# Stick-breaking heads: three places of scores and a look-ahead of two units, one shared bank for two outputs, projections in 256-token pieces through one bank

## The chip, the core and the metric

The kernel runs on one core of one Trainium2 chip. The metric is the device time of one execution in microseconds (us). The kernel before was run three times: 2854.28, 2857.3 and 2858.99 us, median 2857.3. The names of the engines in every profile line are: PE = TensorE (matrix products), PEld = its weight loads, DVE = VectorE, ACT = ScalarE, POOL = GpSimd, SP = SyncE, which issues DMAs.

## The reference

One decoder layer, 2048 tokens of width 1024, float32. One projection feeds eight stick-breaking heads of width 64 and four differential heads; then come an output projection and a SwiGLU feed-forward block. What the change touches is the first kind of head:

```python
h = rmsnorm(x, attn_norm_g[layer])
proj = h @ w_in[layer]
sb_q, sb_k, sb_v, d_q, d_k, d_v = jnp.split(proj, [...])
...
def stick_breaking_attention(q, k, v):
    for start in range(0, S, Q_BLOCK):
        end = start + Q_BLOCK
        z = einsum('bhqd,bhkd->bhqk', q[:, :, start:end], k[:, :, :end]) * scale
        past = arange(end)[None, :] < arange(start, end)[:, None]
        log_beta = log_sigmoid(z)
        log_1m = where(past, log_sigmoid(-z), 0.0)
        acc = cumsum(log_1m, axis=3, reverse=True) - log_1m
        w = where(past, exp(log_beta + acc), 0.0)
        outs.append(einsum('bhqk,bhkd->bhqd', w, v[:, :, :end]))
```

Each weight is a sigmoid times the product of the (1 - beta) of all later keys. The kernel takes the product itself with a scan that runs from the last key backwards, and it carries the running product from one block of keys to the earlier one.

## The kernel before

Every product of two float32 matrices is done with each factor split into a high and a low half-precision part: `mm3` gives three matmuls (high x high, high x low, low x high) into one PSUM sum. The heads are worked in groups of two: groups 0 to 3 are stick-breaking, groups 4 to 7 differential (`SBP` is 4).

**Units.** A stick-breaking group has 40 units. A unit (`unit_sb`) is 128 queries against a block of up to 512 keys, for both heads. Its `scores` are 6 matmuls of 512 columns on PE into a place of 1024 float32 columns of PSUM. Its `main` has three sigmoids on ScalarE (L800 all of beta, L801 and L802 the two halves of 1 - beta; L802 writes back into PSUM), on VectorE two scans (L805) and a product (L808, the last reader of the score place), then a small carry (L813), and on GpSimd a large product (L816). Two units later ScalarE casts the weights to their high part (L829), three units later VectorE makes the low part (L834), both are transposed by DMA, and six units after its `main` PE multiplies two units' weights with v (`values`). At the end of a row of blocks `store` reads the output place (L869 on ScalarE, L870 on VectorE).

**PSUM.** It has eight banks of 512 float32 columns, and is one tile, `psum`, of 4096 columns. The table `places` (L237) gives, for each mode, the columns of the scores ("z"), of projections ("pj") and of outputs ("av"); `place` takes them in turn. The mode is "first" while the input is read, "sb" through groups 0 to 3, "next" from the first projection of a differential group on (set in `project_diff`), "leave" from unit 9 of group 4 and "diff" from its unit 12.

**Projections as filler.** While a group's units run, q, k and v of the next group (or of this one's later tokens) are made between them. `project_sb` makes them for 512 tokens in one place: q 24 matmuls of 512 columns, k the same, v 96 of 128 columns. It is a generator: each `yield` is a point at which it can be left, and `yield END` ends a piece. A finished piece is evacuated by `halved`, ScalarE first (L544, high part) and VectorE behind it (L545, low part from PSUM and the high part), which `clock.at(1, ..., "mid")` puts into the next unit, behind that unit's `main`.

**The order of one unit** in the main loop, the same on all engines since each engine takes its instructions in program order: outputs and stores that are due, `main(n)`, the evacuations ("mid"), the casts and other due work, then `look_ahead(n)`, which puts out scores up to unit n + 1 for stick-breaking groups (n + 2 for differential ones), and then at most one piece of projections if the plan wants PE work by now (`short`). Before the first scores of a new group, what is left of the filler for it is put out, with `tick()` running the due work between pieces.

Of the kernel before, what the change touches and what calls it, by code (L numbers as in the profile page):

```python
# [18 lines left out]
KB = D // 128  # L19
# [5 lines left out]
SBP = 4  # L25
# [39 lines left out]
def hybrid_layer_kernel(  # L65
# [23 lines left out]
    clock = Ticks()  # L89
# [79 lines left out]
    def mm3(ps, lh, ll, rh, rl, first, last):  # L169
        mm(ps, lh, rh, first, False)  # L170
        mm(ps, lh, rl, False, False)
        mm(ps, ll, rh, False, last)
# [52 lines left out]
    with ExitStack() as actx:  # L225
# [9 lines left out]


        places = {  # L237
# [5 lines left out]
        mode, turn = ["first"], {}  # L243

        def place(kind, w):
            if kind == "av1":

                turn[kind] = 128 - turn.get(kind, 0)
                n = turn[kind] + (3840 if turn["pj"] % 2 == 0 else 3328)
                return psum[:, n:n + w]  # L250
            ps = places[mode[0]][kind]
            n = turn[kind] = (turn.get(kind, -1) + 1) % len(ps)
            return psum[:, ps[n]:ps[n] + w]
# [4 lines left out]
        h_hi = hT_p.tile([128, KB, S], F16, name="h_hi")  # L258
        h_lo = hT_p.tile([128, KB, S], F16, name="h_lo")
# [131 lines left out]
        qkv = {g: {} for g in range(NG)}  # L391

        END, DONE = "end", "done"
# [28 lines left out]
        def pj_tile(name):  # L422
            return place("pj", 256)
# [23 lines left out]
        def bank_totals():  # L447
            while totals:
                sp, then = totals.pop(0)

                def read(sp=sp, then=then):
                    sp.take()
                    chain.extend(sp.steps())
                    clock.at(2, then)

                sp.total(pj_tile("tot")[:, 0:1])
                clock.at(1, read, "ev")
                yield END
# [84 lines left out]
        def halved(ps, hi, lo):  # L543
            nc.scalar.activation(hi, ps, AF.Copy, scale=OUT_SC)  # L544
            nc.vector.scalar_tensor_tensor(lo, ps, OUT_SC, hi, ALU.mult, ALU.subtract)  # L545

        def by_parity(k):

            return k.rearrange("p (r n) -> p r n", r=2)

        def project_sb(c, g):


            cs = slice(c * 512, (c + 1) * 512)
            q = qp.tile([128, 2, 2, 512], F16, tag="q", name="q")[:, 0]
            k = kp.tile([128, 2, 512], F16, tag="k", name="k")
            v = vp.tile([128, 4, 2, 128], F16, tag="v", name="v")
            yield from weights(g)
            ws = wsl[g]
            for t in range(2):  # L560
                yield from bank_totals()
                ps, w2 = place("pj", 512), ws[t]
                for kk in range(KB):
                    mm3(ps, w2[:, 0, kk, :], w2[:, 1, kk, :], h_hi[:, kk, cs], h_lo[:, kk, cs],
                        kk == 0, kk == KB - 1)
                    if kk % 2 == 1 and kk < KB - 1:
                        yield

                def evac(ps=ps, t=t):
                    if t == 0:  # L570
                        halved(ps, q[:, 0], q[:, 1])
                    else:
                        halved(ps.rearrange("p (n r) -> p r n", r=2), by_parity(k[:, 0]),
                               by_parity(k[:, 1]))

                clock.at(1, evac, "mid")
                yield END
            yield from bank_totals()
            w2 = ws[2]
            ps = place("pj", 512).rearrange("p (j n) -> p j n", j=4)  # L580
            for j in range(4):

                ts = slice(c * 512 + j // 2 * 256 + j % 2, c * 512 + j // 2 * 256 + 256, 2)
                for kk in range(KB):
                    mm3(ps[:, j, :], h_hi[:, kk, ts], h_lo[:, kk, ts], w2[:, 0, kk, :],
                        w2[:, 1, kk, :], kk == 0, kk == KB - 1)
                if j < 3:
                    yield

            def evac_v():  # L590
                halved(ps, v[:, :, 0, :], v[:, :, 1, :])
                qkv[g][c] = (q, k, v)

            clock.at(1, evac_v, "mid")
            yield END

        staged, roping = [0], [False]

        def project_diff(c, g):
            q = qp.tile([128, 2, 2, 512], F16, tag="q", name="q")  # L600
            k = kp.tile([128, 2, 512], F16, tag="k", name="k")
            v = vp.tile([128, 4, 2, 128], F16, tag="v", name="v")
            yield from weights(g)
            ws = wsl[g]
            if mode[0] == "sb":
                mode[0] = "next"
            while not settle():
                yield END
            while staged[0] == 2:
# [36 lines left out]
            r = {}  # L646
# [568 lines left out]
        def look_ahead(n):  # L1215

            while ahead[0] < len(plan):
                g = plan[ahead[0]][0]
                if ahead[0] > n + (1 if g < SBP else 2):
                    break  # L1220
                if g > 0 and ahead[0] > 0 and plan[ahead[0] - 1][0] != g:
                    for _ in fills[g - 1]:
                        tick()
                plan[ahead[0]][1]()
                ahead[0] += 1
# [4 lines left out]
        for n, (g, scores, front, main, goal, due) in enumerate(plan):  # L1230
            if g != g0:
                base, fbase, g0, since = pe[0], filled[0], g, 0
            since += 1
            if g == SBP and since in (9, 12):
                mode[0] = "leave" if since == 9 else "diff"
            clock.run("ev")
            if front is not None and (n == 0 or plan[n - 1][0] != g):
                front()
            if n + 1 < len(plan) and plan[n + 1][0] == g and plan[n + 1][2] is not None:
                plan[n + 1][2]()  # L1240
            for kind in ("", "main", "mid", None):
                main() if kind == "main" else clock.run(kind)

            def short():
                return pe[0] - base < goal or filled[0] - fbase < due

            look_ahead(n)
            if g == NG - 1 and since == 18:
                late[0] = True
            left = 1 if g + 1 < NG else 2  # L1250
            while left and short() and (n + 2 >= len(plan) or plan[n + 2][0] == g):
                more = fill_next(g)
                if more is DONE:
                    break
                left -= more == END
            clock.step()
# [511 lines left out]
```

## Time and profile before

| what | value |
|---|---|
| median of three runs | 2857.3 us |
| the profiled execution, its own time | 2850.8 us |
| its span, from the first to the last instruction | 2849.0 us |
| mean granted TensorE clock, share of full speed | 0.96 |
| stage: input and first projections | about 0 to 83 us |
| stage: stick-breaking groups 0 to 3 | 83 to 751 us |
| stage: differential groups 4 to 7 | 751 to about 1440 us |
| stage: output projection and norm, then feed-forward | about 1440 us to the end |

A line of a group or timeline view names the line of the kernel, the engine, the operation and `out<-in` by the program's tile names. In the timeline a row begins with its start in us and its duration, and a bracket gives the wait ahead of it and who ended it. In the table of waits a row reads: who waits, for whom, then the sum in us, the number of waits and the longest. In the view by stretches, each engine's busy time is followed by its number of instructions in brackets, and then come the granted clock, the DMA engines' mean busy share and GB/s. The releaser is the semaphore that came last; it is inferred.

### The profile page before, as it was taken

How to read it: one execution, taken by the hardware profiler on the slowest of the kernel's cores; microseconds unless marked ns; L12 is line 12 of the kernel's file. 1: busy time of each engine (PE TensorE's matmuls, PEld its weight loads, DVE VectorE, ACT ScalarE, POOL GpSimd, SP SyncE). 2: the span in 40 equal slices, each digit the busy share in tenths (PEclk: the TensorE clock that was granted, in tenths of full speed). 3: DMA queues.
4: the chain of work that ended last, by engine and by line, in shares of the span. 5: the costliest groups of instructions: out<-in, count | busy, mean ns of one | idle time of the engine just before them, and what ended most of it. 6: DMA issues, size and time to landing. Idle time of an engine off the chain costs nothing.

```text
span 2849.0 us, 50446 instructions
## 1 busy us (share of the span) xinstructions
PE 2527.5 (89%) x19626; PEld 1462.0 (51%) x19626; DVE 2304.0 (81%) x3561; ACT 1549.2 (54%) x2603; POOL 1400.7 (49%) x1099
## 2 busy tenths in 40 slices
PE   6978888897786887877998999999999999999999
PEld 4534445455575666765853444444444444444444
DVE  7898989888889888988748688988777767776776
ACT  5788888886565766565415444545433433343332
POOL 2454545547656565564124555655444544454442
PEclk9989999998898998998998999999999999999999
DMA  4576878866555556668766122122217521112111
GB/s 160 92 146 119 147 138 141 142 129 123 103 94 99 98 105 116 130 120 181 171 159 148 65 100 85 64 78 78 71 45 148 163 89 45 45 49 85 45 45 74
DMA packets 734096, 301.49 MB, mean 106 GB/s; under 512 B 618656, under 2 KB 713120, under 8 KB 733856
## 3 DMA queue, kind: packets, MB, share of 16 engines
q1 hardware_dynamic: 733712, 298.23, 46.4%
q8 instruction: 153, 2.51, 0.4%
q14 instruction: 87, 0.71, 0.1%
q0 software_dynamic: 144, 0.03, 0.0%
HBM read 127.27 MB, written 28.31 MB: 55 GB/s over the span
## 4 chain that ended last, share of the span: by engine, by line
PE 45%; DVE 20%; ACT 6%; POOL 5%; issue 5%; DMA 4%; SPq 1%; DVEq 0%; ACTq 0%; POOLq 0%
PE pw L167 34%; PE psum L167 11%; DMA wt<-wh 2%; DVE fs L1376 2%; DVE mx L178 2%; DVE acc_a L1633 2%; DVE wh L178 1%; DVE pp L178 1%; DVE hh L1420 1%; DVE pp L805 1%; DVE wh L834 1%; ACT pp L930 1%; POOL sc L1550 1%; DVE wmx L105 1%; DVE rt L681 1%
## 5 line engine op out<-in xcount | busy, mean ns | idle before, releaser
L167 PE MATMUL pw<-t,fs 128*128 128x512 f16 x3696 | 808.5, 381 | 15.7 <-issue 10.3
L167 PEld LDWEIGHTS <-fs 128*128 128x128 f16 x3696 | 360.6, 98 | 454.6 <-issue 17.1
L816 POOL TENSOR_TENSOR pp<-pp 128x1024 f32<-128x1024 f32 (+1 forms) x160 | 325.1, 2032 | 317.5 <-DVE pp L813 137.3
L167 PE MATMUL pw<-acc_b,at 128*128 128x512 f16 x2112 | 463.3, 379 | 18.2 <-DVE cg L1558 11.9
L167 PE MATMUL psum<-k,q 64*128 64x512 f16 (+4 forms) x1600 | 288.6, 377 | 152.2 <-DVE pp L808 79.2
L167 PE MATMUL psum<-ws,h_hi 128*128 128x128 f16 x4096 | 377.7, 224 | 21.4 <-ACT psum L1008 12.0
L167 PE MATMUL psum<-ws,h_lo 128*128 128x128 f16 x2048 | 366.9, 224 | 0.0
L167 PEld LDWEIGHTS <-h_hi 128*128 128x128 f16 x4096 | 328.6, 101 | 51.3 <-issue 40.1
L167 PEld LDWEIGHTS <-at 128*128 128x128 f16 x2112 | 205.7, 98 | 267.9 <-issue 22.7
L1561 POOL TENSOR_TENSOR cg<-cg,cu 128x512 f32<-128x512 f32 x88 | 112.4, 1277 | 371.1 <-ACT cg L1560 336.9
L1375 ACT ACTIVATE fs<-acc_b,fst 128x512 f16<-128x512 f32 x264 | 176.1, 714 | 216.8 <-POOL acc_b L1364 143.6
L1633 DVE SCALAR_TENSOR_TENSOR acc_a<-pw,isd,acc_a 128x512 f32<-128x512 f32 x352 | 248.8, 745 | 53.8 <-PE pw L167 53.2
L1376 DVE SCALAR_TENSOR_TENSOR fs<-acc_b,fst,fs 128x512 f16<-128x512 f32 x264 | 248.4, 981 | 31.8 <-ACT fs L1375 31.7
L1550 POOL TENSOR_TENSOR sc<-sc 128x512 f32<-128x512 f32 x132 | 220.0, 1683 | 91.5 <-ACT sc L1544 91.5
L805 DVE TENSOR_TENSOR_SCAN pp<-pp,psum 128x256 f32<-128x256 f32 (+1 forms) x320 | 195.8, 653 | 57.7 <-ACT psum L802 57.0
L167 PEld LDWEIGHTS <-q 64*128 64x128 f16 (+1 forms) x1600 | 94.7, 99 | 260.8 <-DVE pp L808 103.8
L1544 ACT COPY sc<-pw 128x512 f32<-128x512 f32 x176 | 100.4, 582 | 217.9 <-PE pw L167 191.4
L834 DVE TENSOR_TENSOR wh<-pp,wh 128x1024 f16<-128x1024 f32 (+1 forms) x160 | 205.9, 1287 | 2.6 <-DMA wt<-wh 2.6
L167 PEld LDWEIGHTS <-h_lo 128*128 128x128 f16 x2048 | 206.3, 101 | 0.0
L930 ACT ACTIVATE pp<-psum,nb,ds_sc 128x1024 f32<-128x1024 f32 (+4 forms) x192 | 183.1, 954 | 18.8 <-DVE pp L178 9.6
L178 DVE TENSOR_REDUCE mx<-psum 128x1 f32<-128x1024 f32 (+4 forms) x192 | 173.6, 905 | 24.1 <-PE psum L167 21.3
L800 ACT ACTIVATE pp<-psum,gsc 128x1024 f32<-128x1024 f32 (+1 forms) x160 | 164.8, 1030 | 36.4 <-PE psum L167 32.4
(211 smaller groups left out, 4456.2 us busy)
## 6 DMA issues: line engine op xcount, KB each, us to landing
acc_b<-in_w_gate_dram SPq DMA_DIRECT2D x22, 1024.0 KB, 5.2
acc_b<-in_w_up_dram SPq DMA_DIRECT2D x22, 1024.0 KB, 7.5
acc_b<-in_w_down_dram SPq DMA_DIRECT2D x22, 1024.0 KB, 9.5
raw<-in_w_in_dram SPq DMA_DIRECT2D x24, 512.0 KB, 4.3
pp<-in_x_dram SPq DMA_DIRECT2D x16, 512.0 KB, 5.2
wt<-wh SPq DMA_TRANSPOSE x512, 3.2
raw<-in_w_o_dram SPq DMA_DIRECT2D x16, 512.0 KB, 4.1
mt<-mix_d SPq DMA_DIRECT2D x32, 256.0 KB, 3.2
```

Of the source, the lines that this page charges most:

```text
L167: nc.tensor.matmul(ps, lhsT=lhsT, rhs=rhs, start=start, stop=stop)
L178: fn(*a, **k)
L800: nc.scalar.activation(be, z[:, :, 0:W], AF.Sigmoid, scale=sc[:, 0:1])
L805: nc.vector.tensor_tensor_scan(ga, ga, z[:, h, P:W][:, ::-1], 2.0 ** 14 if diag else cx[a][:, h, 0:1], ALU.mult, ALU.mult)
L816: nc.gpsimd.tensor_mul(b4, b4, gp[:, :, 1:P + 1].rearrange("p h (r n) -> p h r n", r=1).to_broadcast([128, 2, 2, P]))
L834: nc.vector.tensor_sub(wl[:, 0:n], b2, u["wh"][:, 0:n])
L930: nc.scalar.activation(pt, u["z"][:, 0:e - b], AF.Exp, scale=ds_sc, bias=nb[:, m:m + 1], accum_out=su[:, jj:jj + 1])
L1375: nc.scalar.activation(w[:, m, 0:4], src, AF.Copy, scale=sw)
L1376: nc.vector.scalar_tensor_tensor(w[:, m, 4:8], src, sw, w[:, m, 0:4], ALU.mult, ALU.subtract)
L1550: nc.gpsimd.tensor_add(s[m], s[m], y[m])
L1561: nc.gpsimd.tensor_mul(g, g, u)
L1633: nc.vector.scalar_tensor_tensor(acc[:, i, hs], ps, pr.isd, acc[:, i, hs], ALU.mult, ALU.add)
```

## The change

The table of places loses the modes "next" and "leave". In mode "sb" the scores have three places of two banks (columns 0, 1024 and 2048), the projections have the two halves of one bank (columns 3072 and 3328), and the outputs the two halves of the last (3584 and 3840). The input's mode has four half-bank places for projections instead of two whole ones. `look_ahead` runs two units ahead in all groups, and mode "diff" begins at unit 9 of group 4. `project_sb` makes q, k and v in two pieces of 256 tokens each, with an `END` and an evacuation for each piece, so a call has six pieces instead of three. Lines from 237 on move by -2, and lines of `unit_sb` by +2, so L800, L802, L805, L808 are L802, L804, L807, L810 afterwards, and L544 and L545 are L542 and L543.

```diff
@@ -235,10 +235,8 @@
 
 
         places = {
-            "first": {"z": [0, 1024, 2048], "pj": [3072, 3584]},
-            "sb": {"z": [0, 1024], "pj": [2048, 2560], "av": [3072, 3584]},
-            "next": {"z": [0, 1024], "pj": [2048, 2560, 2304, 2816], "av": [3072, 3584]},
-            "leave": {"z": [0, 1024], "pj": [3072, 3584]},
+            "first": {"z": [0, 1024, 2048], "pj": [3072, 3584, 3328, 3840]},
+            "sb": {"z": [0, 1024, 2048], "pj": [3072, 3328], "av": [3584, 3840]},
             "diff": {"z": [0, 1024, 2048], "pj": [3072, 3584]}}
         mode, turn = ["first"], {}
 
@@ -558,41 +556,47 @@
             yield from weights(g)
             ws = wsl[g]
             for t in range(2):
+                for u in range(2):
+                    yield from bank_totals()
+                    ps, w2 = pj_tile("pj"), ws[t]
+                    us = slice(c * 512 + u * 256, c * 512 + u * 256 + 256)
+                    for kk in range(KB):
+                        mm3(ps, w2[:, 0, kk, :], w2[:, 1, kk, :], h_hi[:, kk, us],
+                            h_lo[:, kk, us], kk == 0, kk == KB - 1)
+                        if kk == KB // 2 - 1:
+                            yield
+
+                    def evac(ps=ps, t=t, u=u):
+                        if t == 0:
+                            halved(ps, *(q[:, y, u * 256:u * 256 + 256] for y in range(2)))
+                        else:
+                            halved(ps.rearrange("p (n r) -> p r n", r=2),
+                                   *(by_parity(k[:, y])[:, :, u * 128:u * 128 + 128]
+                                     for y in range(2)))
+
+                    clock.at(1, evac, "mid")
+                    yield END
+            w2 = ws[2]
+            for u in range(2):
                 yield from bank_totals()
-                ps, w2 = place("pj", 512), ws[t]
-                for kk in range(KB):
-                    mm3(ps, w2[:, 0, kk, :], w2[:, 1, kk, :], h_hi[:, kk, cs], h_lo[:, kk, cs],
-                        kk == 0, kk == KB - 1)
-                    if kk % 2 == 1 and kk < KB - 1:
+                ps = pj_tile("pj").rearrange("p (j n) -> p j n", j=2)
+                for j in range(2):
+
+                    ts = slice(c * 512 + u * 256 + j, c * 512 + u * 256 + 256, 2)
+                    for kk in range(KB):
+                        mm3(ps[:, j, :], h_hi[:, kk, ts], h_lo[:, kk, ts], w2[:, 0, kk, :],
+                            w2[:, 1, kk, :], kk == 0, kk == KB - 1)
+                    if j == 0:
                         yield
 
-                def evac(ps=ps, t=t):
-                    if t == 0:
-                        halved(ps, q[:, 0], q[:, 1])
-                    else:
-                        halved(ps.rearrange("p (n r) -> p r n", r=2), by_parity(k[:, 0]),
-                               by_parity(k[:, 1]))
-
-                clock.at(1, evac, "mid")
+                def evac_v(ps=ps, u=u):
+                    js = slice(2 * u, 2 * u + 2)
+                    halved(ps, v[:, js, 0, :], v[:, js, 1, :])
+                    if u == 1:
+                        qkv[g][c] = (q, k, v)
+
+                clock.at(1, evac_v, "mid")
                 yield END
-            yield from bank_totals()
-            w2 = ws[2]
-            ps = place("pj", 512).rearrange("p (j n) -> p j n", j=4)
-            for j in range(4):
-
-                ts = slice(c * 512 + j // 2 * 256 + j % 2, c * 512 + j // 2 * 256 + 256, 2)
-                for kk in range(KB):
-                    mm3(ps[:, j, :], h_hi[:, kk, ts], h_lo[:, kk, ts], w2[:, 0, kk, :],
-                        w2[:, 1, kk, :], kk == 0, kk == KB - 1)
-                if j < 3:
-                    yield
-
-            def evac_v():
-                halved(ps, v[:, :, 0, :], v[:, :, 1, :])
-                qkv[g][c] = (q, k, v)
-
-            clock.at(1, evac_v, "mid")
-            yield END
 
         staged, roping = [0], [False]
 
@@ -602,8 +606,6 @@
             v = vp.tile([128, 4, 2, 128], F16, tag="v", name="v")
             yield from weights(g)
             ws = wsl[g]
-            if mode[0] == "sb":
-                mode[0] = "next"
             while not settle():
                 yield END
             while staged[0] == 2:
@@ -1216,7 +1218,7 @@
 
             while ahead[0] < len(plan):
                 g = plan[ahead[0]][0]
-                if ahead[0] > n + (1 if g < SBP else 2):
+                if ahead[0] > n + 2:
                     break
                 if g > 0 and ahead[0] > 0 and plan[ahead[0] - 1][0] != g:
                     for _ in fills[g - 1]:
@@ -1231,8 +1233,9 @@
             if g != g0:
                 base, fbase, g0, since = pe[0], filled[0], g, 0
             since += 1
-            if g == SBP and since in (9, 12):
-                mode[0] = "leave" if since == 9 else "diff"
+            if g == SBP and since == 9:
+
+                mode[0], turn["pj"] = "diff", 0
             clock.run("ev")
             if front is not None and (n == 0 or plan[n - 1][0] != g):
                 front()
```

Three places show how this changes the order on the engines. In each row stand the line, the operation, `out<-in` and the shape; a bracket names the semaphores that it waits for. First PE, near the end of group 0, where the scores of a unit (from `k,q`) are followed by a piece of a projection (from `h_hi`, `h_lo` and the weights `ws`). Before:

```order
L167 LDWEIGHTS q
L167 MATMUL psum<-k,q 128x512
L167 LDWEIGHTS ws
L167 MATMUL psum<-h_hi,ws 128x512
L167 LDWEIGHTS ws
L167 MATMUL psum<-h_lo,ws 128x512
```

And the changed kernel at the same place:

```order
L167 LDWEIGHTS q
L167 MATMUL psum<-k,q 128x512
L167 LDWEIGHTS ws
L167 MATMUL psum<-h_hi,ws 128x256 [waits DVE_49]
L167 LDWEIGHTS ws
L167 MATMUL psum<-h_lo,ws 128x256
```

The piece has half the columns, and its first matmul has a wait for VectorE that was not there. The second place is VectorE at the end of group 0; `q`, `k`, `v` are evacuations, `pp` and `wh` the units' work. Before, the last evacuation of this stretch:

```order
L805 SCALAR_TENSOR_TENSOR pp<-pp,psum 128x256 x2
L808 TENSOR_TENSOR pp<-pp,psum 128x2x256
L834 TENSOR_TENSOR wh<-pp,wh 128x1024
L813 TENSOR_REDUCE pp<-pp 128x2
L545 SCALAR_TENSOR_TENSOR v<-psum,v 128x4x128
```

And in the changed kernel, two units of the same stretch:

```order
L810 TENSOR_TENSOR pp<-pp,psum 128x2x256
L836 TENSOR_TENSOR wh<-pp,wh 128x1024
L815 TENSOR_REDUCE pp<-pp 128x2
L543 SCALAR_TENSOR_TENSOR q<-psum,q 128x256
L807 SCALAR_TENSOR_TENSOR pp<-pp,psum 128x256 x2
L810 TENSOR_TENSOR pp<-pp,psum 128x2x256
L836 TENSOR_TENSOR wh<-pp,wh 128x1024
L815 TENSOR_REDUCE pp<-pp 128x2
L543 SCALAR_TENSOR_TENSOR k<-psum,k 128x2x128
```

The evacuation that PE's next piece waits for stands, as before, behind the scans and the product of the unit in which it is put out; there are now two for every 512 tokens of q, k or v. The third place is ScalarE in the same stretch, the sigmoids of a unit, what stands behind them, and the next unit's first sigmoid. Before:

```order
L800 ACTIVATE pp<-psum,gsc 128x1024 [waits DVE_49,PE_49]
L801 ACTIVATE pp<-psum,gsc 128x2x256 [waits DVE_49]
L802 ACTIVATE psum<-psum,gsc 128x2x256 [waits Activation_49]
L544 ACTIVATE q<-psum 128x512 [waits PE_49]
L829 CAST wh<-pp 128x1024 [waits DMAHW1_49,Pool_49]
L800 ACTIVATE pp<-psum,gsc 128x1024 [waits DVE_49,PE_49]
```

And in the changed kernel:

```order
L802 ACTIVATE pp<-psum,gsc 128x1024 [waits DVE_49,PE_49]
L803 ACTIVATE pp<-psum,gsc 128x2x256 [waits DVE_49]
L804 ACTIVATE psum<-psum,gsc 128x2x256 [waits Activation_49]
L542 ACTIVATE q<-psum 128x256 [waits PE_49]
L831 CAST wh<-pp 128x1024 [waits DMAHW5_49,Pool_49]
L802 ACTIVATE pp<-psum,gsc 128x1024 [waits DVE_49]
```

The order on ScalarE is the same, with a piece's evacuation ahead of the cast and of the next unit's sigmoids. The last rows are the end of group 0 in the changed kernel, where the pieces of group 1 that are left over are put out between the last sigmoids of group 0 and the first of group 1:

```order
L542 ACTIVATE k<-psum 128x2x128 [waits DVE_49,PE_49]
L831 CAST wh<-pp 128x1024 [waits DMAHW1_49,Pool_49]
L871 ACTIVATE mxs<-psum 128x256 [waits PE_49]
L831 CAST wh<-pp 128x1024 [waits DMAHW3_49,Pool_49]
L542 ACTIVATE k<-psum 128x2x128 [waits DVE_49,PE_49]
L831 CAST wh<-pp 128x1024 [waits DMAHW5_49,Pool_49]
L542 ACTIVATE v<-psum 128x2x128 [waits DVE_49,PE_49] x2
L802 ACTIVATE pp<-psum,gsc 128x1024
```

Three pieces (the second `k` and two of `v`) stand there with no unit between them; before, every piece of group 1 was put out between units.

## The prediction

> **What bounds the kernel now.** I read the page first, then busy time by stretch for the four groups of stick-breaking heads, then the table of waits for the same stretch, then the timeline inside it.
>
> ```profile
> span 2849.0 us, 50446 instructions
> PE 2527.5 (89%) x19626; PEld 1462.0 (51%) x19626; DVE 2304.0 (81%) x3561; ACT 1549.2 (54%) x2603; POOL 1400.7 (49%) x1099
> 83.00:239.00 156.00, 126.48 (x1203) 71.03 (x1200) 138.36 (x249) 131.06 (x183) 79.54 (x39) 0.92 0.68 124
> 239.00:398.00 159.00, 134.42 (x1283) 75.08 (x1283) 143.59 (x246) 131.77 (x184) 79.92 (x40) 0.92 0.74 138
> 398.00:551.00 153.00, 130.17 (x1283) 75.02 (x1283) 140.16 (x242) 131.10 (x184) 80.49 (x41) 0.96 0.79 142
> 551.00:751.00 200.00, 159.81 (x1906) 110.55 (x1907) 171.46 (x280) 140.10 (x204) 116.93 (x70) 0.90 0.71 128
> ```
>
> The four stretches (columns after the length: PE, PEld, DVE, ACT, POOL busy, granted clock, DMA share, GB/s) are groups 0 to 3, 40 units each, 668 us together. The shares of the page do not hold here: over the whole span PE is the busy engine, but in these stretches it is VectorE, with 138.4 + 143.6 + 140.2 + 171.5 = 593.6 us of 668. VectorE idles 74 us; that is the most that any smoothing could win. What it waits for:
>
> ```profile
> PE psum L167 <- DVE pp L808: 79.2, 50, 5.5
> DVE pp L805 <- ACT psum L802: 57.0, 49, 4.6
> ACT pp L800 <- PE psum L167: 32.4, 28, 5.1
> ACT q L544 <- PE psum L167: 15.6, 6, 4.2
> ACT v L544 <- PE psum L167: 11.9, 8, 3.3
> ACT k L544 <- PE psum L167: 8.5, 5, 3.0
> PE psum L167 <- DVE v L545: 3.1, 4, 1.2
> ```
>
> 57 of the 74 us are waits for the third sigmoid (L802), and ScalarE in turn waits 68 us for PE: 32.4 us for scores and 36.0 us for projections that it is to evacuate. PE waits for VectorE's last read of a score place (L808), and almost never (3.1 us) for an evacuation. How a late projection becomes a late sigmoid stands in ScalarE's rows where pieces are dense:
>
> ```profile
> 200.55 1.04 ACT L829 CAST wh<-pp 128x1024 f16<-128x1024 f32 x1
> 201.49 1.12 ACT L800 ACTIVATE pp<-psum,gsc 128x1024 f32<-128x1024 f32 x1
> 202.50 0.69 ACT L801 ACTIVATE pp<-psum,gsc 128x512 f32<-128x512 f32 x1
> 203.22 0.66 ACT L802 ACTIVATE psum<-psum,gsc 128x512 f32<-128x512 f32 x1
> 206.39 0.60 ACT L544 ACTIVATE v<-psum 128x512 f16<-128x512 f32 x1 [2.51 <-PE psum L167]
> 206.88 1.04 ACT L829 CAST wh<-pp 128x1024 f16<-128x1024 f32 x1
> 208.61 1.11 ACT L800 ACTIVATE pp<-psum,gsc 128x1024 f32<-128x1024 f32 x1 [0.69 <-PE psum L167]
> ```
>
> ScalarE works in order. At 203.88 it has nothing to wait for but the projection; it stands 2.51 us in front of the evacuation, and the cast and the next unit's sigmoids stand behind it.
>
> **The change, part by part.** (1) A third score place and a look-ahead of two units: PE may put scores(n+2) out before unit n's place is free. This can remove what the 57 us hold. (2) Projections in pieces of 256 tokens: the longest stretch of PE work between two scores halves. (3) The price: both pieces now lie in one PSUM bank (columns 3072 and 3328). In the instruction order the first matmul of a piece waits for VectorE's evacuation of the piece before it, although that lies in the other half; in before, two banks took turns and pieces of one unit and the next started without a wait. 73 pieces of the four groups carry this wait on an evacuation that stands behind the same unit's own VectorE work; in before 15 pieces wait, all on the unit before.
>
> What the wait does is a chain over two units, each step from a row:
>
> ```profile
> 491.89 0.68 DVE L545 SCALAR_TENSOR_TENSOR k<-psum,k 128x512 f16<-128x512 f32 x1
> 492.62 0.27 PE L167 MATMUL psum<-ws,h_hi 128*128 128x128 f16 x2 [1.32 <-DVE k L545]
> 522.11 0.28 PE L167 MATMUL psum<-ws,h_hi 128*128 128x128 f16 x2
> 524.74 0.22 PE L167 MATMUL psum<-ws,h_lo 128*128 128x128 f16 x1
> 524.89 0.82 PE L167 MATMUL psum<-k,q 64*128 64x512 f16 x6
> 633.35 0.38 ACT L544 ACTIVATE v<-psum 128x256 f16<-128x256 f32 x1 [0.29 <-PE psum L167]
> 633.63 1.04 ACT L829 CAST wh<-pp 128x1024 f16<-128x1024 f32 x1
> 666.35 0.41 DVE L545 SCALAR_TENSOR_TENSOR v<-psum,v 128x256 f16<-128x256 f32 x1
> 666.68 1.37 DVE L805 TENSOR_TENSOR_SCAN pp<-pp,psum 128x256 f32<-128x256 f32 x2
> ```
>
> VectorE's evacuation ends, PE starts 0.05 us later (492.57 to 492.62); a piece of 48 matmuls of 128 columns takes 2.7 us (522.11 to the scores at 524.89, 2.78); ScalarE starts its evacuation, about 0.1; 0.28 until the cast behind it (633.35 to 633.63); the cast 0.94 (200.55 to 201.49); three sigmoids 2.39 (201.49 to 203.88): 0.05 + 2.7 + 0.1 + 0.28 + 0.94 + 2.39 = 6.46 us until VectorE can begin unit n+2. Meanwhile it has unit n+1 and the piece's evacuation:
>
> ```profile
> 521.80 1.38 DVE L805 TENSOR_TENSOR_SCAN pp<-pp,psum 128x256 f32<-128x256 f32 x2
> 523.10 0.67 DVE L808 TENSOR_TENSOR pp<-pp,psum 128x512 f32<-128x512 f32 x1
> 523.67 1.22 DVE L834 TENSOR_TENSOR wh<-pp,wh 128x1024 f16<-128x1024 f32 x1
> 524.81 0.15 DVE L813 TENSOR_REDUCE pp<-pp 128x2 f32<-128x2 f32 x1
> 524.88 0.68 DVE L545 SCALAR_TENSOR_TENSOR k<-psum,k 128x512 f16<-128x512 f32 x1
> 525.47 1.26 DVE L805 TENSOR_TENSOR_SCAN pp<-pp,psum 128x256 f32<-128x256 f32 x2
> ```
>
> 3.08 us for the unit (521.80 to 524.88) and 0.33 for a half evacuation (666.35 to 666.68) are 3.41. So VectorE stands 6.46 - 3.41 = 3.0 us, and no score place helps: the sigmoids are behind the evacuation on ScalarE. Where full pieces follow unit upon unit, one such gap covers two units: 9.9 us for two, against 8.1 in a PE-bound pair (two pieces 5.4, two scores 1.4, values 1.4).
>
> Counting by the order: 56 of the 73 are whole pieces done in one unit; they stand in runs that give 9 + 9 + 10 + 9 = 37 gaps in groups 0 to 3: 37 x 3.0 = **111 us**. The other 17 begin with a half, and their evacuation comes a unit later: from nothing to 1.7 us each, I take 1.0, **17 us**. At the end of group 0, three pieces are left over and are put out one behind the other with no unit between (in before that happens only after group 3); PE work 8 us plus three evacuations of about 1 us, less what VectorE still has: **10 us**, from 5 to 14. VectorE's other idle time, 74 - 57 = **17 us**, stays. Against this, weight preparation and rope on VectorE, some 117 us that are not unit work (593.6 less 128 full units x 3.08, 32 short ones at 1.8, 42 evacuations x 0.59), fall into gaps for a part: 37 gaps on 160 units, **-27 us** (from 0 to -50). Smaller evacuations: 42 times 2 x 0.33 - 0.59 = 0.07, **+3 us**.
>
> New stretch: 593.6 + 3 + 111 + 17 + 10 + 17 - 27 = 725 us against 668, **+57 us**. The scores are never late in this sum; what (1) can win is already counted, since none of the 57 us is left in it.
>
> Outside the four groups:
>
> ```profile
> 60.72 0.38 PE L167 MATMUL psum<-h_hi,ws 128*128 128x512 f16 x1
> 65.90 1.04 PE L199 MATMUL psum<-ident,pp 128*128 128x128 f32 x8
> PE psum L167 <- ACT pp L930: 8.0, 4, 4.2
> ```
>
> In the input loop a projection of 512 tokens takes 5.18 us (60.72 to 65.90), and the loop ends one every second row block; with 256 it ends half of that, and six pieces of 2.6 us come behind the loop while the loop is up to 13 us shorter: 0 to +5, I take +3. PE's 768 extra matmuls cost nothing if 256 columns hide the weight load, as 128 columns do above. In the first units of group 4 (751 to 790) PE waits 8.0 us for exponentials with two score places; the third saves 0 to 8, I take -3. Together nothing.
>
> The profiled execution took 2850.8 us, 6.5 below the median of 2857.3. The sum changes it to 2908; on the median it is 2857 + 57 = **2914 us**.
>
> **A rule against the change.** The order says that a piece waits for the other half of its bank; no run here yet shows how long. [...]
>
> **The rivals.** (a) *Faster*: PE gets to the piece later than the evacuation is done, so the new wait ends nothing. For: PE is 81 to 87% busy here, and the 79.2 us for L808 vanish. It decides if PE is 3.0 us behind VectorE at a piece's start; but a whole piece, scores and half a value step are 2.7 + 0.7 + 0.7 = 4.1 us against 3.41 + gap, so PE has caught up every second unit. If it holds everywhere, 57 us go and 3 come: 2803; in half of the places, about 2830. (b) *Much slower*: PE's clock drops in the waits.
>
> ```profile
> 150.00:200.00 50.00, 36.24 (x261) 17.54 (x263) 48.95 (x84) 42.12 (x57) 28.63 (x14) 0.78 0.76 144
> ```
>
> Where units run without projections the granted clock is already 0.78. If each waiting piece ran at half speed it would take 2.7 us more: 37 x 2.7 = 100, 3014 us. [...] (c) *No change*: gaps half as many and preparation work filling them, 2851 to 2863.
>
> **How the numbers follow.** Forecast 0.72 (2880 to 2965), (a) 0.14, (b) 0.08, (c) 0.06. The forecast's own ends come from the gap (37 x 2 to 37 x 3.3), the halves (0 to 29), the drain and the filling. The range from 2850 to 2970 leaves out (a) and most of (b). 0.2% is 6 us, about what a measurement of this kernel can tell from no change: faster 0.14, same 0.05, slower 0.81.
>
> **What would show it.** In the changed trace: PE waiting for the evacuation (L543) some 100 us instead of 3; ScalarE waiting for PE in front of L542 some 90 us instead of 36; VectorE waiting for L804 above 110 us instead of 57; PE's wait for L810 near nothing; units in pairs of about 10 us where whole pieces follow each other; 10 us without sigmoids at the end of group 0; groups 0 to 2 about 15 us longer each. I am wrong if PE's wait for L543 is small, or if sigmoids start on time behind pieces that waited.

## The result, and the profile after

The changed kernel takes 3037.2 us (median; 3033.11 to 3037.93), the kernel before 2857.2 us in the same runs: ratio 1.0627, 95% interval 1.0611 to 1.0643. It is slower by 180 us, where 57 were forecast; the direction was right and the time lies 67 us above the range. One of the ten runs of the twelfth experiment below took 4318 us at a granted clock of 0.56; its figures there leave it out.

The page of the changed kernel, its span and busy times, and then the view by stretches with a stretch for each stick-breaking group (columns as before: PE, PEld, DVE, ACT, POOL busy, granted clock, DMA share, GB/s):

```profile
span 3036.1 us, 52027 instructions
PE 2588.2 (85%) x20394; PEld 1576.5 (52%) x20394; DVE 2297.4 (76%) x3609; ACT 1553.7 (51%) x2651; POOL 1394.2 (46%) x1099
82.00:282.00 200.00, 145.07 (x1446) 99.98 (x1444) 144.53 (x265) 132.92 (x195) 77.71 (x39) 0.86 0.59 108
282.00:487.00 205.00, 144.32 (x1437) 101.52 (x1436) 136.27 (x258) 132.80 (x197) 77.70 (x40) 0.86 0.56 99
487.00:699.00 212.00, 150.59 (x1475) 105.98 (x1475) 142.30 (x255) 132.26 (x196) 80.57 (x41) 0.82 0.59 105
699.00:931.00 232.00, 166.07 (x1966) 128.77 (x1966) 161.29 (x272) 137.56 (x205) 113.92 (x68) 0.84 0.55 101
```

All of it is in the four groups: 849 us from the first sigmoid to the first sigmoid of the last unit, where the kernel before has 663 (83 to 746), 186 of the span's 187. VectorE has about the same work (584.4 us busy, before 590.6) and idles 265 us instead of 72. PE has the same products to make and is busy longer: these four stretches add up to 606 us, the kernel before has 549.

The same stretch of both kernels and of two experiments below, each as one row:

```profile
83.00:746.00 663.00, 549.10 (x5650) 330.33 (x5647) 590.62 (x1007) 531.36 (x747) 356.34 (x187) 0.92 0.72 133
```
```profile
82.00:931.00 849.00, 606.05 (x6321) 436.25 (x6317) 584.39 (x1048) 535.54 (x789) 349.89 (x187) 0.85 0.57 103
```
```profile
84.00:845.00 761.00, 578.87 (x6321) 420.78 (x6317) 583.48 (x1049) 535.36 (x789) 349.06 (x187) 0.89 0.64 115
```
```profile
84.00:735.00 651.00, 549.19 (x6323) 398.62 (x6320) 593.51 (x1050) 537.73 (x789) 352.74 (x187) 0.93 0.76 135
```

The first is the kernel before, the second the changed one, the third the changed one with an earlier store (first experiment), the fourth the kernel before with small pieces in two banks (fourth experiment). Length less VectorE's busy time is VectorE's idle time: 72, 265, 178 and 57 us. The change makes the stretch 186 us longer and VectorE's idle time 192 us longer.

What waits for what, in the table of waits of the changed kernel for the four groups (82 to 931 us):

```profile
ACT mxs L871 <- PE psum L167: 119.0, 29, 12.6
DVE pp L807 <- ACT psum L804: 111.4, 80, 3.6
DVE mxs L872 <- ACT mxs L871: 90.2, 23, 7.5
PE psum L167 <- DVE pp L810: 57.0, 21, 6.9
ACT q L542 <- PE psum L167: 54.3, 16, 6.0
PE psum L167 <- DVE v L543: 50.8, 17, 7.9
ACT v L542 <- PE psum L167: 48.9, 19, 5.3
ACT k L542 <- PE psum L167: 42.0, 17, 6.2
PE psum L167 <- DVE q L543: 40.3, 20, 5.6
PE psum L167 <- DVE wsw L145: 26.1, 8, 5.6
PE psum L167 <- DVE k L543: 26.0, 16, 5.3
```

The forecast's wait is there: PE waits 50.8 + 40.3 + 26.0 = 117 us for the evacuation, and the 26 us that the view puts down to L145 are of the same kind (tenth experiment). But the first and third row were in no term of the forecast. L871 and L872 are the **store** of an output: ScalarE stands 119 us in front of it, VectorE 90. In the kernel before this table has no such row. The timeline of the changed kernel shows one such place (PE's rows between the piece's first and the values are left out):

```profile
323.19 0.42 DVE L543 SCALAR_TENSOR_TENSOR v<-psum,v 128x256 f16<-128x256 f32 x1
323.66 0.37 PE L167 MATMUL psum<-ws,h_hi 128*128 128x128 f16 x2 [3.03 <-DVE v L543]
...
328.87 1.73 PE L167 MATMUL psum<-wt,v 128*64 128x256 f16 x24
330.64 0.38 ACT L871 ACTIVATE mxs<-psum 128x256 f16<-128x256 f32 x1 [9.47 <-PE psum L167]
330.92 1.11 ACT L802 ACTIVATE pp<-psum,gsc 128x1024 f32<-128x1024 f32 x1
332.64 0.66 ACT L804 ACTIVATE psum<-psum,gsc 128x512 f32<-128x512 f32 x1
333.34 1.27 DVE L807 TENSOR_TENSOR_SCAN pp<-pp,psum 128x256 f32<-128x256 f32 x2 [1.85 <-ACT psum L804]
```

VectorE's evacuation ends, PE's piece starts, the values of the **next** row follow it, and only when these have ended does ScalarE read the finished row, in the other half of the bank; the unit's sigmoids stand behind that read. From the evacuation to VectorE's next scan 9.7 us pass for a single unit. Without the store this chain covers two units (the evacuation on ScalarE stands behind a unit's sigmoids, the store ahead of them).

### The profile page after: what moved, and what is told of

It reads as the page before. It is cut to its first block, busy times and chain, and to the rows that moved or that the text cites. A ratio compares the mean times of both kernels' runs of the same rounds, so it can differ in the third digit from the quotient of the medians.

```text
span 3036.1 us, 52027 instructions
## 1 busy us (share of the span) xinstructions
PE 2588.2 (85%) x20394; PEld 1576.5 (52%) x20394; DVE 2297.4 (76%) x3609; ACT 1553.7 (51%) x2651; POOL 1394.2 (46%) x1099
## 4 chain that ended last, share of the span: by engine, by line
PE 49%; DVE 25%; ACT 10%; issue 6%; POOL 5%; DMA 4%; SPq 0%; DVEq 0%; ACTq 0%; POOLq 0%
PE pw L167 32%; PE psum L167 17%; DVE wh L836 3%; ACT pp L802 2%; DVE pp L807 2%; DVE mx L178 2%; DVE fs L1379 2%; DVE pp L178 2%; DVE acc_a L1636 2%; DMA wt<-wh 2%; DVE pp L810 1%; DVE wh L178 1%; ACT pp L803 1%; ACT wh L831 1%; DVE hh L1423 1%
## 5 line engine op out<-in xcount | busy, mean ns | idle before, releaser
L167 PE MATMUL psum<-ws,h_hi 128*128 128x128 f16 x4096 | 398.1, 230 | 83.8 <-DVE v L543 35.9
L167 PEld LDWEIGHTS <-h_hi 128*128 128x128 f16 x4096 | 342.2, 104 | 116.9 <-issue 105.3
L167 PE MATMUL psum<-ws,h_lo 128*128 128x128 f16 x2048 | 386.2, 230 | 0.0
L167 PE MATMUL psum<-h_hi,ws 128*128 128x256 f16 x1024 | 212.8, 304 | 87.9 <-DVE q L543 40.3
L807 DVE TENSOR_TENSOR_SCAN pp<-pp,psum 128x256 f32<-128x256 f32 (+1 forms) x320 | 196.2, 654 | 112.7 <-ACT psum L804 111.4
L167 PEld LDWEIGHTS <-ws 128*128 128x128 f16 x1536 | 164.9, 108 | 139.9 <-issue 107.2
L167 PEld LDWEIGHTS <-h_lo 128*128 128x128 f16 x2048 | 213.2, 104 | 0.0
L836 DVE TENSOR_TENSOR wh<-pp,wh 128x1024 f16<-128x1024 f32 (+1 forms) x160 | 199.0, 1244 | 2.1 <-DMA wt<-wh 2.1
```

Of the source, the lines that this page charges most:

```text
L167: nc.tensor.matmul(ps, lhsT=lhsT, rhs=rhs, start=start, stop=stop)
L807: nc.vector.tensor_tensor_scan(ga, ga, z[:, h, P:W][:, ::-1], 2.0 ** 14 if diag else cx[a][:, h, 0:1], ALU.mult, ALU.mult)
L836: nc.vector.tensor_sub(wl[:, 0:n], b2, u["wh"][:, 0:n])
```

## The experiments

Each is an edit to one of the two kernels, or to an earlier experiment; times are medians, the kernel before was run beside them at 2857.6 to 2859.4 us.

**1. The store ahead of the next row's values** (in the changed kernel):

```diff
-                    clock.at(2, store, "")
+                    clock.at(1, store, "")
```

> The changed kernel with one edit: the store of an output is due one unit after the last values instead of two, so that it stands ahead of the next row's values in the order. Theory S (the shared output bank): in the changed kernel ScalarE's store waits for PE's values of the next row, in the other half of the bank, 106 us in 28 waits, and these stand behind a piece that waited for VectorE; the sigmoids stand behind the store. With the store ahead of those values the wait at L871 falls below 15 us and the time to between 2900 and 2945 us (the 57 us of the prediction's chain, which stays). Rival P (the wait for the evacuation alone makes the loss, the store only shows it): the waits move from L871 to L542 and L804, and the time stays above 2990.

2952.5 us, ratio 1.0320 (1.0294 to 1.0346): 85 us less than the changed kernel, 94 more than before. The waits from 84 to 845 us, the same stretch of units:

```profile
DVE pp L807 <- ACT psum L804: 102.6, 69, 3.6
ACT q L542 <- PE psum L167: 52.3, 17, 6.7
ACT v L542 <- PE psum L167: 51.0, 21, 7.2
ACT k L542 <- PE psum L167: 40.5, 14, 5.8
ACT mxs L871 <- PE psum L167: 10.2, 6, 3.5
```

The store's wait falls from 119 to 10 us, below the 15 expected (the expectation's 106 us leave out the last store, 12.6 us), and it does not move to L542 or L804, which stay about as they were. Theory S holds; the time is 7 us above its range, so the remaining chain is dearer than the forecast's 57.

**2. Shared outputs alone** (in the kernel before; the same in the mode "next"):

```diff
-            "sb": {"z": [0, 1024], "pj": [2048, 2560], "av": [3072, 3584]},
+            "sb": {"z": [0, 1024], "pj": [2048, 2560], "av": [3072, 3328]},
```

> The kernel before with one edit: both output places lie in one bank (columns 3072 and 3328); pieces of 512 in two banks, two score places and look-ahead of one unit stay. Theory S: the store on ScalarE waits for the next row's values, which stand on PE behind a whole piece of up to 5.2 us: 31 stores by 1.5 to 3.5 us, +45 to +110 us, waits at L869 from near 0 to 40 us or more. Rival P: without a wait for the evacuation PE is early enough, within 10 us of before.

2897.7 us, ratio 1.0129 (1.0107 to 1.0150), +40 us, a little under the range of theory S and far from rival P. One edit to a table makes a wait of ScalarE that did not exist:

```profile
DVE pp L805 <- ACT psum L802: 79.8, 73, 2.9
ACT mxs L869 <- PE psum L167: 67.4, 26, 8.9
DVE mxs L870 <- ACT mxs L869: 19.2, 10, 5.6
```

In the changed kernel the same sharing costs 85 us. The timeline above shows at one place what is added there, a piece ahead of the values that waits itself; no run separates that part of the 85 us.

**3. Pieces of 256 in one bank** and **4. pieces of 256 in two banks** (both the kernel before with the changed `project_sb`; the third has this edit besides):

```diff
-            "sb": {"z": [0, 1024], "pj": [2048, 2560], "av": [3072, 3584]},
+            "sb": {"z": [0, 1024], "pj": [2048, 2304], "av": [3072, 3584]},
```

> The kernel before with the changed project_sb (pieces of 256) and both piece places in one bank (columns 2048 and 2304) in the mode of the first four groups; outputs in two banks, two score places, look-ahead of one unit. The prediction's chain (each piece waits for the evacuation of the one before, which stands behind VectorE's unit): +30 to +75 us, PE's wait for L543 or its like 60 us or more. By theory S the greater part of the 180 us isn't here, so under +90. Rival P: +120 or more.

> The kernel before with the changed project_sb (pieces of 256), piece places in two banks as before. Both theories: the size of the pieces by itself costs little, -10 to +15 us; no wait of PE for an evacuation beyond 15 us in all. If it costs 30 us or more, smaller pieces (768 more matmuls, and half as much filler per unit) are a cause of their own.

One bank: 2956.4 us, ratio 1.0343 (1.0320 to 1.0366), +98. Two banks: 2842.9 us, ratio 0.9943 (0.9927 to 0.9959), -15, a little more than the -10 expected at most. So the column 2304 instead of 2560, nothing else, costs 113 us. No expectation of the third held: it is above the chain's +75 and theory S's +90 and below rival P's +120, and with the small pieces' own gain the bank costs nearly what that rival said. PE's wait for the evacuation is there, 82 us in its table of waits. The smaller pieces are a gain by themselves; here VectorE idles least of the four rows above (57 us), PE hardly waits for an evacuation (4.3 us of idle time ahead of the q and k pieces, last section), and the sigmoid's wait falls:

```profile
PE psum L167 <- DVE pp L814: 58.8, 36, 5.4
DVE pp L811 <- ACT psum L808: 47.9, 47, 7.0
```

(L814 and L811 are the product and the scans in this kernel's numbering; before, these waits were 79.2 and 57.0.)

**5. Look-ahead of one unit** (the first experiment with the old limit):

```diff
-                if ahead[0] > n + 2:
+                if ahead[0] > n + (1 if g < SBP else 2):
```

> The changed kernel with the early store, and a look-ahead of one unit for stick-breaking heads as before (the third score place stays in turn). The prediction's step 'no score place helps, the sigmoids stand behind the evacuation on ScalarE': within 12 us of the early store with look-ahead two (2952), so 2940 to 2965. If the second unit of look-ahead does win something under these waits, 2975 or more.

2965.4 us, ratio 1.0377 (1.0356 to 1.0399): 13 us more than with two units, just above the range and below the 2975 set for the other case. The second unit of look-ahead is worth about 13 us under these waits, not nothing.

**6. The evacuations ahead of the low parts on VectorE** (the first experiment, with a place of their own for both evacuations):

```diff
-                    clock.at(1, evac, "mid")
+                    clock.at(1, evac, "out")
...
+                clock.run("out")
                 clock.run("low")
```

> The changed kernel with the early store, and the evacuations of stick-breaking projections put ahead of the low parts (L836) and the carry on VectorE, behind the scans and the product; ScalarE's order stays but for other late work. Theory C (the chain evacuation - piece - evacuation - cast - sigmoids sets the rhythm of two units): PE starts each waiting piece about 1.4 us earlier, two units take 8.8 us instead of 9.9, 37 times 1.1 = 40 us less than 2952, so 2900 to 2930. If the wait for the evacuation isn't what decides, 2942 to 2962.

2905.2 us, ratio 1.0166 (1.0143 to 1.0189): 47 us less, where the chain's arithmetic gave 40. Moving the evacuation past one instruction of 1.2 us and a short one on VectorE, with no change of work, brings back half of the 94 us that were left; the chain from evacuation to piece sets the rhythm there. The ninth experiment is the check without that chain.

**7. Pieces in pairs**, in groups 0 to 2 two in every second unit (the first experiment, with):

```diff
             left = 1 if g + 1 < NG else 2
+            if g < SBP - 1:
+                left = 2 if since % 2 == 0 else 0
```

> The changed kernel with the early store, and in groups 0 to 2 up to two pieces in every second unit instead of one in each, all through the same one bank. Theory C: a pair's first piece waits for evacuations put out one unit earlier, done by then, and the wait of the chain is gone in these groups: 90 to 130 us less than 2952, so 2820 to 2870; PE's waits for L543 below 35 us in all. If sharing the bank costs by itself (access, not order), 2930 or more.

2928.8 us, ratio 1.0242 (1.0220 to 1.0264): only 24 us less. The expectation missed twice: PE still waits 62 us for L543 (87 in the first experiment, expected below 35), and the table of waits has a new kind of row, ScalarE waiting for VectorE's evacuation of the other half.

```profile
ACT q L542 <- DVE v L543: 15.2, 4, 5.3
ACT k L542 <- DVE q L543: 14.7, 6, 3.4
ACT k L542 <- DVE k L543: 12.4, 4, 3.6
ACT v L542 <- DVE v L543: 8.3, 3, 3.5
ACT v L542 <- DVE k L543: 5.4, 2, 4.3
```

Both only read PSUM, in different halves; still the second half's read on ScalarE waits for the first half's read on VectorE, and so it stands, with the sigmoids behind it, behind VectorE's unit. With a sixth row of 4.3 us these are 60 us.

**8. Shared outputs with the early store** (the second experiment with the edit of the first):

> The kernel before with both output places in one bank and the store one unit earlier. Theory S (only the order of the store behind the next row's values costs): back to the kernel before, 2850 to 2868. If two halves of a bank in use at once cost by themselves, it stays near 2890 to 2900.

2856.2 us, ratio 0.9991 (0.9982 to 1.0001): no difference from before. Two outputs in one bank cost nothing here; the order of one read behind the other half's writes does (2897.7 us in the second experiment).

**9. Two banks, evacuations ahead of the low parts** (the fourth experiment with the edit of the sixth):

> The kernel of small pieces in two banks (two score places, look-ahead of one, outputs in two banks), with the evacuations of stick-breaking projections ahead of the low parts on VectorE. Theory C: this order won 47 us only because a piece waited for the evacuation; with two banks none waits, so within 8 us of 2843. If an earlier evacuation helps by itself (ScalarE, q/k/v earlier), 2830 or less.

2840.1 us, ratio 0.9932 (0.9914 to 0.9951): as expected no different from 2842.9. The edit that won 47 us with one bank wins nothing where no piece waits.

**10. The weight totals in a bank of their own** (the third experiment; totals of weight maxima take a turn in the pieces' bank):

```diff
         def pj_tile(name):
+            if name == "tot" and mode[0] == "sb":
+                return psum[:, 2560:2816]
             return place("pj", 256)
```

> The kernel of small pieces in one bank (two score places, outputs in two banks, 2956 us), with the 14 totals of weight maxima in a bank of their own (column 2560, free in that mode) instead of in the pieces' bank. Theory T: a total is one more link in the chain, since it waits for an evacuation and the next piece waits for its reading (PE waits 18 us for L145 there): 10 to 40 us less, 2916 to 2946. If totals only fill time that the chain leaves over, 2950 to 2962.

2953.3 us, ratio 1.0336 (1.0312 to 1.0359), 3 us from the third: theory T falls. PE's wait named L145 did not go either (24.7 us). The releaser was a wrong name: in the changed kernel's timeline an evacuation stands right ahead of such an instruction,

```profile
348.16 0.42 DVE L543 SCALAR_TENSOR_TENSOR q<-psum,q 128x256 f16<-128x256 f32 x1
348.49 0.15 DVE L145 TENSOR_SCALAR wsw<-wsw 128x1 int32<-128x1 int32 x1
348.63 0.37 PE L167 MATMUL psum<-h_hi,ws 128*128 128x256 f16 x1 [5.64 <-DVE wsw L145]
```

and PE starts 0.05 us after the evacuation's end (348.58), before L145 has ended (348.64). At all eight such places of the changed kernel's four groups an evacuation ends 0.05 us before PE starts, so these are waits for evacuations too.

**11. Pairs with ScalarE's parts first** (the seventh; the two instructions of `halved` due at two places):

```diff
-                    clock.at(1, evac, "mid")
+                    clock.at(1, lambda abc=abc: part_hi(*abc), "mid")
+                    clock.at(1, lambda abc=abc: part_lo(*abc), "mid2")
...
-            for kind in ("", "main", "mid", None):
+            for kind in ("", "main", "mid", "mid2", None):
```

> The pieces in pairs (2929 us), with the evacuations cut in two: ScalarE's high parts of all pieces that are due first, then VectorE's low parts. In the pairs ScalarE's evacuation of the second half waits 60 us for VectorE's evacuation of the first half, the same bank, and the sigmoids stand behind it. Theory C (any order across engines within one bank, also between two readers, is what costs): 33 such waits become 11 and 30 to 60 us go, 2870 to 2900. If those waits only stand where ScalarE would wait anyway, 2918 to 2940.

2882.8 us, ratio 1.0085 (1.0061 to 1.0108), 46 us less, within theory C's range. No wait of ScalarE for an evacuation on VectorE is left in its table.

**12. The same, ahead of the low parts** ("out" and "out2" in place of "mid" and "mid2", run ahead of "low"):

> The same, with both parts ahead of the low parts of the weights (L836) and the carry on VectorE, which won 47 us without pairs. With pairs a piece rarely waits for an evacuation of the same unit, so little more is left: 0 to 25 us less than the run before it in this list. Theory C with the third score place at work: 2835 to 2890. If it isn't below the small pieces in two banks (2843), the third score place doesn't pay for what its two banks take away, in this order.

2857.7 us, ratio 1.0011 (0.9996 to 1.0026), 25 us less, the end of the expected range. With the store early, pieces in pairs, and the readers in a good order, the layout of the change is level with the kernel before, and 15 us above the small pieces in two banks (2842.9). In this order the third score place, with its two banks, does not pay for what it takes away.

## Why the prediction was right or wrong

**The bound and the direction were right.** VectorE's waits set the four groups, and its work did not change (590.6 to 584.4 us). Chance for slower was 0.81. Two readings are off by little and move nothing: PE is 80 to 85% busy in the prediction's four stretches, not 81 to 87%, and the three terms of a PE-bound pair add up to 8.2 us, not 8.1.

**The step that failed: the output bank.** The price (3) of the prediction spoke of "both pieces" in one bank and put the order by bank into the sum for projections alone. The two outputs share a bank in the same line of the diff, and the sum has no term for the store: forecast nothing, measured 85 us (3037.2 to 2952.5, first experiment). For the outputs alone the order by bank is worth 40 us in the second experiment and nothing in the eighth, where the store's place alone differs. The prediction applied it to one bank of two. The instruction rows had shown L871 with a wait for PE; the question not asked was for which matmul. Without this wait the change stands at 2952.5 us, inside the forecast's range.

**The chain of pieces was right in kind and too small.** The prediction's chain is what the third, fourth and sixth experiments show: 113 us for one bank against two, PE's waits for the evacuation 117 us in the changed kernel, 143 with those named L145 (forecast some 100), 47 us back by an earlier evacuation. But the sum for it was +57, and the changed kernel without the store's wait has +94. VectorE's idle time of the first experiment, 178 us, can be set against the forecast's 111 + 17 + 10 + 17 - 27 = 128. In front of the scans (L807) it waits 102.6, and in front of its own evacuation (L543) 40 us for L542: 143 where the gaps, halves and the drain were to give 138. The other waits are 35 instead of 17, and nothing is left to set against the 27 us that weight preparation was to absorb. Whether these 27 us were not absorbed, or longer gaps made up for them, the account can't tell; the next paragraph shows that gaps were longer.

**One price in the chain was wrong: 2.7 us for a piece.** A place of the changed kernel:

```profile
572.41 0.41 DVE L543 SCALAR_TENSOR_TENSOR k<-psum,k 128x256 f16<-128x256 f32 x1
572.87 0.37 PE L167 MATMUL psum<-h_hi,ws 128*128 128x256 f16 x1 [4.91 <-DVE k L543]
...
578.08 1.03 PE L167 MATMUL psum<-k,q 64*128 64x512 f16 x6
578.19 0.39 ACT L542 ACTIVATE k<-psum 128x256 f16<-128x256 f32 x1 [5.27 <-PE psum L167]
578.47 1.04 ACT L831 CAST wh<-pp 128x1024 f16<-128x1024 f32 x1
578.61 0.42 DVE L543 SCALAR_TENSOR_TENSOR k<-psum,k 128x256 f16<-128x256 f32 x1 [2.98 <-ACT k L542]
579.40 1.12 ACT L802 ACTIVATE pp<-psum,gsc 128x1024 f32<-128x1024 f32 x1
581.13 0.66 ACT L804 ACTIVATE psum<-psum,gsc 128x512 f32<-128x512 f32 x1
581.83 1.39 DVE L807 TENSOR_TENSOR_SCAN pp<-pp,psum 128x256 f32<-128x256 f32 x2 [2.80 <-ACT psum L804]
```

It is the chain as forecast, step by step, but the piece takes 5.2 us (572.87 to 578.08) and the whole 9.0 instead of 6.46. This is rival (b) in some of the places: over this piece the granted clock is 0.50; over the piece from 585.38 to 588.15, behind a wait of 0.85 us, it is 1.00. In the four groups of the first experiment the timeline has 81 whole pieces of 256 tokens that run without a break: 21 of them take 4.0 to 5.3 us, and 20 of these stand behind a wait of 2 us or more; nearly all the others take about 2.8. The 20 are together 36 us longer than 2.8 us each, 1.8 us a piece, and PE is busy 30 us longer than in the two-bank kernel with the same matmuls (578.9 and 549.2). That is about the 37 us between 57 and 94; that they are the missing ones is argued, not shown, since no run changes the clock alone. The 2.7 us that rival (b) put on each of 37 pieces, and its chance of 0.08, were the author's estimates: no row beside them shows half speed, though the kernel before has a granted clock of 0.50 from 150 to 155 us, inside the stretch that was read as 0.78.

**The third score place.** "No score place helps" was nearly right: the second unit of look-ahead is worth 13 us (fifth experiment). But PE's wait for the last reader of a place, to be "near nothing", is still 57 us (before 79).

**The smaller pieces.** The sum had +3 us for more evacuations and nothing for the gain; alone they win 15 us (fourth experiment). That they shorten PE's longest stretch between two scores was named in (2) and not priced. That the gain comes from there is not shown.

**Other marks.** VectorE's wait for L804 is 111 us, as forecast (above 110). ScalarE's wait in front of L542 is 145 us instead of some 90. Groups 0 to 2 grew by 44 to 59 us each instead of 15. The end of group 0, from the first sigmoid of the last unit but one to that of group 1's first unit, is 22 us instead of 8: +14, forecast 10. Rival (a), that the new waits end nothing, fell.

## What to carry to other kernels

When two tiles are put into one PSUM bank, go through every reader of either half, not only the ones that the change moves, and ask which instruction of the other half stands ahead of it in the program; what mattered here is what was queued behind that reader (a unit's sigmoids behind a store that waited 119 us in the changed kernel). For the outputs here, sharing cost nothing once each read stood ahead of the other half's next write (2856.2 us; 2897.7 without that), and a due time of one unit earlier was the whole difference. A bank taken from a buffer in turn was a price in order (113 us for the pieces in one bank), to be set against the place gained: a half-size piece in two banks (2840 to 2843 us) beat both kernels, and a third score place did not pay in any order that was run.

## What the runs showed of the hardware

PE's speed fell behind its waits, and the slow pieces made others wait longer (ScalarE 5.27 us at 578.19 above). The same 896 matmuls of 256 columns, in the changed kernel and in the small pieces in two banks, as groups of the four stretches (the mean in ns is the second number behind the bar):

```profile
L167 PE MATMUL psum<-h_hi,ws 128*128 128x256 f16 x896 | 189.2, 306 | 87.9 <-DVE q L543 40.3 <-DVE k L543 16.1 <-DVE wsw L145 16.0
```
```profile
L167 PE MATMUL psum<-h_hi,ws 128*128 128x256 f16 x896 | 160.4, 276 | 4.3 <-DVE q L545 1.7 <-DVE k L545 1.3 <-DVE v L545 0.8
```

The granted clock is 0.85 there and 0.93 here. The mean hides two speeds. Pieces behind waits of 3.03 and 4.91 us (above) took 5.2 us at a granted clock of 0.50; one of the changed kernel behind a wait of 0.85 us took 2.8 at 1.00 (585.38 to 588.15). In the first experiment 58 of the 59 whole pieces behind a shorter wait than 2 us, or none, took under 4 us; of the 22 behind longer ones 20 took 4.0 to 5.3 and two 2.8. One of them, with the scores before its wait and the values behind it (PE's rows between the first and the values are left out):

```profile
726.78 0.82 PE L167 MATMUL psum<-k,q 64*128 64x512 f16 x6
729.96 0.27 PE L167 MATMUL psum<-ws,h_hi 128*128 128x128 f16 x2 [2.36 <-DVE v L543]
...
734.36 1.50 PE L167 MATMUL psum<-wt,v 128*64 128x256 f16 x24
```

The scores ahead of the wait ran at the faster speed (0.82 us; in the changed kernel, behind a wait of 2.45 us, the same six took 1.46 at a granted clock of 0.50, at 319.17, and 0.82 at 1.00, at 567.14), PE had no other wait of over 0.3 us in the 9 us before, and the piece took 4.4 us.

In the same first experiment a piece behind a wait of 2.69 us took 2.7 us (547.89 to 550.61); what decides between the two speeds no run shows.
